# Gated linear attention: one head per half of the array's rows for scores and state, one product per decay level for q and k together, the output gate read from PSUM

## The chip, the cores and the metric

The kernel runs on one core of a Trainium2 chip, as one launch. The metric is the device time of that launch in microseconds (us). The engines are TensorE (PE, matrix products), VectorE (DVE), ScalarE (ACT), GpSimd (POOL) and SyncE (SP, which here issues transfers). Each has its own instruction stream, and semaphores order them. A tile is spread over 128 partitions; PE writes its results to PSUM, which has eight banks.

## The reference

One step of a layer with two groups of heads side by side, followed by a feed-forward part:

```
n = rmsnorm(x);  z = n @ w_in
A = windowed attention with sinks          (8 heads)
B = gated linear attention (GLA)           (4 heads, 64 keys by 128 values)
h = x + concat(A, B) @ w_out
y = h + relu(rmsnorm(h) @ w_up)^2 @ w_down
```

The change is in the GLA. Per chunk, with `g` the log of the forget gate of each key channel:

```
b     = cumsum(g)
o     = (q * exp(b)) @ S + A @ v
A[t,s] = sum_k q[t,k] * k[s,k] * exp(b[t,k] - b[s,k])   for s <= t
S_new = exp(b[-1]) * S + (k * exp(b[-1] - b))^T @ v
out   = rmsnorm_per_head(o) * g_gla_out * silu(rg)
```

There are 2048 prompt tokens (16 tiles of 128) and 32 sample tokens (tile 16, which runs first).

## The kernel before, in words

The program has three phases: projections and attention to about 401 us, the GLA (`gla_phase`) from there to about 772 us, then the output projection and the feed-forward part. The GLA goes through eight halves h of two tiles (the first also has the sample tile). Per half PE projects q and k (`zq`, `zk`: four results of 24 products with 256 columns, `gla_cols`), `decay` makes the running sum `cc` of the log gates, and per tile PE projects v (`zv`: 24 products with 512 columns).

Two heads lie one above the other on the 128 partitions (64 key channels each), and there are two such pairs p. `gla_tile` handles one tile:

- L767 and L772: `qkp` = q * k (the diagonal of A) and `Qc` = q * exp(b), on DVE.
- The decay factors. For each level m of 64, 32, ... 1 the tokens are cut into blocks of 2m, and the score of a row in the second half of a block against a column in its first half is factored at the block's middle. POOL makes the exponents of the two halves of the blocks apart (L788, L789) and those of the state update (L779) in tiles `E` of four levels; ACT takes the exponential in place (L113).
- DVE then multiplies q by E into `Qb` (L798, 14 instructions per tile, one for each level and head, 64 partitions each). `Qb` is block-diagonal: each head's part lies beside zeros, so that one product over all 128 rows gives two heads. DVE also multiplies E by k in two instructions of 1024 columns (L804).
- PE: `dg` (the diagonal), `kdp` (transposes for the state update), then the scores `A0`, `A1`: 26 products, in tiles of 128 rows by 64 columns, 64 moving columns each (128 for m = 64). Each f32 product is two instructions in the trace.
- DVE copies the scores under a mask into `AT` (L863, `copy_predicated`, 12 per tile); ACT does the level m = 64 (L856).
- PE: `go` (the output: `Qc` times the state with 256 columns, `AT` times v with 128) and `dS` (L879 to L890); DVE updates the state `Sp` (L896, four instructions on 64 partitions); ACT copies and squares the output (L901, L902), DVE sums the squares (L904), takes the inverse root (L170 to L175) and multiplies into the gate `g` (L909, four instructions); PE transposes it (`gTp`), and a transfer takes it out.

The order of the work: tasks (`gla_tile`, `decay`) are generators that yield for so many ns on a clock of PE work that the builder keeps (`_pe`, `tick`, `finish`), so PE's instructions stand in the order in which the builder emits them, and a PE instruction that waits holds all behind it. The other engines' orders are set by a scheduler. PSUM has three banks for the wide projections and five for everything else in this phase (`ps_s`), handed out in turn: a new tile waits until the last reader of the one five before it is done. `reach` and `after` make a tile wait in the builder for a stage of an earlier one.

Of the kernel before, what the change touches and what calls it, by code (L numbers as in the profile page):

```python
# [13 lines left out]
ALU = mybir.AluOpType  # L14
# [14 lines left out]
class Builder:  # L29
# [630 lines left out]
    def gla_phase(self):  # L660
        tc, a, V, S, G, Q = self.tc, self.a, self.V, self.S, self.G, self.Q
        nt = self.nt
        with ExitStack() as ctx:
# [7 lines left out]
            for key in ("p", "s"):  # L671
                St[key] = c.tile([P, 2, 2, P], F32, tag=f"S{key}", name=f"S{key}")
                G.memset(St[key], 0.0)
            Qb = [c.tile([P, 7, 2, 2, 64], F32, tag=f"Qb{i}", name=f"Qb{i}") for i in range(2)]
            for x in Qb:
                G.memset(x, 0.0)
            for p in range(2):
                for hh in range(2):
                    Q.dma_start(St["s"][hh * 64 : hh * 64 + 64, p, hh, :], a["state_gla"][2 * p + hh])

            halves = self.halves
            vs, gs, vready, cnt, glas, stage, decs = {}, {}, set(), [0], [], {}, {0: self.dec0}
# [18 lines left out]
            def project(h):  # L701
# [3 lines left out]
                qg = wk.tile([P, 2, 288], F32, tag="qg", name=f"qg_{h}")  # L705
                kg = wk.tile([P, 2, 288], F32, tag="kg", name=f"kg_{h}")
                for wt, dst, sc, nm in ((self.wqg, qg, 0.125, "q"), (self.wkg, kg, 1.0, "k")):
                    for p in range(2):
                        if h == 0 and self.head0:
                            ps = self.head0.pop(0)  # L710
                        else:
                            ps = self.gla_cols(wt, p, f"z{nm}_{h}_{p}", rh, rl, N)
                        V.scalar_tensor_tensor(out=dst[:, p, :N], in0=ps, scalar=sc, in1=rb[:, :N], op0=ALU.mult, op1=ALU.mult)
# [5 lines left out]
                offs = np.cumsum([0] + [self.rows(t) for t in tiles])  # L719

                for i, t in enumerate(tiles):
                    r = self.rows(t)
                    if i < 2:
                        n = len(glas)
                        reach(n - 2, 2)
                        glas.append(None)
                        glas[n] = self.spawn(gla_tile(n, t, int(offs[i]), qg, kg, self.cc[h]), 0 if i else 0)
                        self.tick()
# [9 lines left out]
                    if i == 2:  # L738
# [3 lines left out]
                        glas[n] = self.spawn(gla_tile(n, t, int(offs[i]), qg, kg, self.cc[h]), 0)  # L742
# [11 lines left out]
            def gla_tile(n, t, off, qg, kg, cc):  # L754
# [5 lines left out]
                q, k, cv = qg[:, :, tk], kg[:, :, tk], cc[:, :, tk]  # L760
# [3 lines left out]
                Qt = Qb[cnt[0] % 2]  # L764
                cnt[0] += 1
# [8 lines left out]
                for gi, g_ in enumerate([list(range(0, 4)), list(range(4, NL + 1))]):  # L774
                    E = wk.tile([P, 4, 2, P], F32, tag="E", name=f"E_{t}_{gi}", bufs=4)
                    for s_, li in enumerate(g_):
                        ev = E[:, s_, :, :L]
                        if li == NL:
# [3 lines left out]
                            continue  # L782
                        m = lv[li]
                        nb = L // (2 * m)
                        c5 = cv.rearrange("q p (n h m) -> q p n h m", h=2, m=m)
                        e5 = ev.rearrange("q p (n h m) -> q p n h m", h=2, m=m)
                        ref = c5[:, :, :, 0, m - 1 : m].broadcast_to([P, 2, nb, m])
# [4 lines left out]
                    for s_, li in enumerate(g_):  # L792
                        if li == NL:
                            continue
                        m = lv[li]
                        for hh in range(2):
                            hp = slice(hh * 64, hh * 64 + 64)
                            (G if li % 4 < 0 else V).tensor_tensor(  # L798
                                out=Qt[hp, li, :, hh, : L // 2].rearrange("q p (n m) -> q p n m", m=m),
                                in0=q[hp].rearrange("q p (n h m) -> q p n h m", h=2, m=m)[:, :, :, 1, :],  # L800
                                in1=E[hp, s_, :, :L].rearrange("q p (n h m) -> q p n h m", h=2, m=m)[:, :, :, 1, :],
                                op=ALU.mult,
                            )
# [26 lines left out]
                for p in range(2):  # L830
                    self.tr(pk[:L, p * P : (p + 1) * P], kd[:, p, :L])
# [4 lines left out]
                for gi, (l0, l1) in enumerate(((0, 3), (3, 7)) if L == P else ((0, NL),)):  # L836
                    ps = self.ps_s(f"A{gi}_{t}")
                    at, c0 = {}, 0
                    for li in range(l0, l1):
                        w = 64 if lv[li] == 64 else L // nh // 2  # L840
                        at[li] = ps[:, c0 : c0 + 4 * w].rearrange("s (p h x) -> s p h x", p=2, h=2)
                        c0 += 4 * w
                        for p in range(2):
                            if w == 64:

                                self.mm(at[li][p * 64 : p * 64 + 64, p], K(li)[:, p, :64], Qt[:, li, p], True, True)
                                continue
                            for a0 in range(nh):
                                r = slice(a0 * 64, a0 * 64 + L // nh)
                                self.mm(at[li][r, p], K(li)[:, p, r], Qt[:, li, p, :, a0 * w : (a0 + 1) * w], True, True)  # L850
                    for li in range(l0, l1):
                        m = lv[li]
                        w = at[li].shape[3]
                        if m == 64:
                            for p in range(2):
                                S.activation(AT[:64, 2 * p : 2 * p + 2, 64:], at[li][p * 64 : p * 64 + 64, p], AF.Copy)  # L856
                            continue
                        for a0 in range(nh):
                            r = slice(a0 * 64, a0 * 64 + L // nh)
                            dst = AT[r, :, r].rearrange("s a (n h m) -> s a n h m", h=2, m=m)[:, :, :, 1, :]  # L860
                            src = at[li][r].rearrange("s p h (n m) -> s (p h) n m", m=m)
                            mk = masks[r, LEVELS.index(m), :w].rearrange("s (n m) -> s n m", m=m)
                            V.copy_predicated(dst, mk.unsqueeze(1).broadcast_to([L // nh, 4, w // m, m]), src)  # L863
                    if l1 < NL:
                        yield 800
# [10 lines left out]
                o = self.ps_s(f"go_{t}")  # L876
                for p in range(2):
                    if not first:
                        self.mm(  # L879
                            o[:L, p * 256 : p * 256 + 256], Qc[:, p, :L], St_[:, p].rearrange("k h v -> k (h v)"), True, False  # L880
                        )
# [523 lines left out]
```

## Time and profile before

| What | Value |
|---|---|
| Three runs, us | 2366.48, 2371.55, 2370.27 (median 2370.27) |
| The profiled execution, us | 2372.48 |
| Its span, us | 2370.7 |
| Granted TensorE clock, mean | 0.979 |
| PE busy over the span | 95% |
| DVE, ACT, POOL busy | 63%, 40%, 50% |

The profiled execution is 2.2 us above the median of the runs; 1.8 us of its time lie around its span. A busy share over the whole span says little here: the phase after 772 us is PE's alone, while in the GLA the engines hand work to each other. The windows view gives busy times by stretch, the waits view what an engine stood still for, the lines view the mean duration of each kind of instruction, the timeline single instructions (a run of equal ones in one row, from the first start to the last end).

### The profile page before, as it was taken

The numbers are of one execution on the slowest core, as the hardware profiler recorded it, in microseconds if no ns is written. First come the engines' busy times: TensorE is split into PE (matmuls) and PEld (weight loads), VectorE is DVE, ScalarE is ACT, GpSimd is POOL, SyncE is SP. The second block draws the span as 40 slices with busy tenths as digits, with TensorE's granted clock in tenths as the row PEclk, the third lists the DMA queues.
The fourth block names the chain that finished last, engine by engine and source line by source line (L and its number), as shares of the span: only waits on it lengthen the run. The fifth ranks groups of instructions, "written<-read, shape, count | busy, mean of one in ns | idle before, by whom it ended". The sixth has DMA issues, their size and how long they took to land.

```text
span 2370.7 us, 38100 instructions
## 1 busy us (share of the span) xinstructions
PE 2246.4 (95%) x14473; PEld 2112.0 (89%) x14473; DVE 1501.8 (63%) x3621; ACT 949.4 (40%) x2011; POOL 1187.1 (50%) x1074
## 2 busy tenths in 40 slices
PE   6999999898877899999999899999999999999999
PEld 4777776687767899999999899999999999999999
DVE  6665656999999755555564755555556665555555
ACT  3554444454543633333334533333334533333331
POOL 3221224333341457766754466666663556666662
PEclk9999999899998999999999999999999999999999
DMA  8864563322322422232226222222226122222221
GB/s 204 159 126 103 129 165 120 82 75 59 102 80 74 121 81 72 81 98 72 72 86 193 80 71 72 72 72 71 71 62 223 35 82 72 72 72 72 72 63 51
DMA packets 214455, 221.45 MB, mean 93 GB/s; under 512 B 38736, under 2 KB 178976, under 8 KB 214272
## 3 DMA queue, kind: packets, MB, share of 16 engines
q1 hardware_dynamic: 214272, 219.02, 33.4%
q8 instruction: 114, 1.87, 0.3%
q14 instruction: 69, 0.57, 0.1%
HBM read 180.08 MB, written 38.91 MB: 92 GB/s over the span
## 4 chain that ended last, share of the span: by engine, by line
PE 76%; DVE 14%; DMA 4%; ACT 2%; issue 1%; POOL 1%; SPq 1%; POOLq 0%; ACTq 0%; DVEq 0%
PE dn L105 30%; PE op L105 6%; PE PS4B L105 4%; PE PA11B L105 4%; PE PA12B L105 4%; PE zq L105 4%; PE PS1T L105 3%; PE PA22T L105 3%; PE PS3T L105 3%; PE PS2T L105 3%; PE zr L105 3%; DVE Qb L798 3%; DVE AT L863 2%; PE zkv L105 2%; PE zv L105 2%
## 5 line engine op out<-in xcount | busy, mean ns | idle before, releaser
L1073 POOL TENSOR_TENSOR wu<-stage,wu 128x512 fp32r<-128x512 f32 x336 | 435.1, 1304 | 514.3 <-ACT wu L1072 514.3
L1240 DVE TENSOR_TENSOR y<-y,dn 128x360 f32<-128x360 f32 (+1 forms) x768 | 392.2, 514 | 221.4 <-PE dn L105 218.4
L1072 ACT ACTIVATE wu<-stage 128x512 fp32r<-128x512 f32 x336 | 205.9, 627 | 491.8 <-PE dn L105 224.7
L1075 POOL TENSOR_TENSOR stage<-stage 128x512 f32<-128x512 f32 x192 | 250.5, 1304 | 7.5
L1193 ACT ACTIVATE r<-PA11B 128x360 f32<-128x360 f32 (+1 forms) x48 | 22.0, 458 | 315.7 <-PE PA11B L105 315.7
L1180 DVE TENSOR_TENSOR PA12B<-PA12B,r 128x360 f32<-128x360 f32 (+1 forms) x48 | 25.3, 527 | 150.2 <-PE PA12B L105 150.2
L105 PE MATMUL PS2T<-T2h,wu 128*128 128x360 f32 (+1 forms) x384 | 100.7, 324 | 13.9 <-ACT T2h L1105 13.9
L699 POOL TENSOR_TENSOR g<-g,ggla 128x512 f32<-128x512 f32 (+1 forms) x17 | 22.8, 1347 | 170.5 <-ACT g L113 170.5
L105 PE MATMUL PA22T<-T4h,wu 128*128 128x360 f32 (+1 forms) x384 | 102.8, 332 | 0.0
L105 PE MATMUL PS4B<-B22h,wu 128*128 128x360 f32 (+1 forms) x384 | 100.0, 324 | 0.0
L105 PE MATMUL PS3T<-T3h,wu 128*128 128x360 f32 (+1 forms) x384 | 99.4, 322 | 0.0
L105 PE MATMUL PS1T<-T1h,wu 128*128 128x360 f32 (+1 forms) x384 | 98.9, 321 | 0.0
L105 PE MATMUL PA11B<-B11h,wu 128*128 128x360 f32 (+1 forms) x384 | 98.8, 321 | 0.0
L105 PE MATMUL PA12B<-B21h,wu 128*128 128x360 f32 (+1 forms) x384 | 98.7, 321 | 0.0
L798 DVE TENSOR_TENSOR Qb<-qg,E 64x128 f32<-64x128 f32 (+1 forms) x234 | 86.7, 370 | 10.5 <-ACT E L113 7.4
L105 PEld LDWEIGHTS PS2T<-T2h,wu 128*128 128x128 f32 x384 | 68.9, 190 | 14.8 <-ACT T2h L1105 14.8
L497 ACT ACTIVATE P<-S,negm 128x192 f32<-128x192 f32 (+2 forms) x128 | 51.5, 417 | 51.7 <-DVE negm L492 34.9
L863 DVE COPY_PREDICATED AT<-masks,A 64x128 f32<-64x128 int32 (+1 forms) x197 | 67.4, 342 | 6.2 <-ACT AT L856 1.2
L105 PEld LDWEIGHTS PA22T<-T4h,wu 128*128 128x128 f32 x384 | 71.2, 196 | 0.0
L105 PEld LDWEIGHTS PS4B<-B22h,wu 128*128 128x128 f32 x384 | 68.9, 190 | 0.0
L105 PEld LDWEIGHTS PS3T<-T3h,wu 128*128 128x128 f32 x384 | 68.6, 189 | 0.0
L105 PEld LDWEIGHTS PS1T<-T1h,wu 128*128 128x128 f32 x384 | 68.1, 188 | 0.0
(1008 smaller groups left out, 7807.0 us busy)
## 6 DMA issues: line engine op xcount, KB each, us to landing
stage<-in_w_up SPq DMA_DIRECT2D x96, 512.0 KB, 3.7
stage<-in_w_down SPq DMA_DIRECT2D x96, 512.0 KB, 3.9
stage<-in_w_out SPq DMA_DIRECT2D x24, 512.0 KB, 4.8
xT1a<-in_xT_prompt SPq DMA_DIRECT2D x16, 512.0 KB, 4.1
stage<-in_w_in SPq DMA_DIRECT2D x16, 512.0 KB, 6.7
x1a<-in_x_prompt SPq DMA_DIRECT2D x16, 512.0 KB, 6.6
out_yT_prompt<-y SPq DMA_DIRECT2D x32, 180.0 KB, 2.6
m<-mixT SPq DMA_DIRECT2D x11, 512.0 KB, 3.9
```

What stands on the lines that cost most here:

```text
L105: self._pe(self.T.matmul(out, lhsT, rhs, start=start, stop=stop), ns)
L497: S.activation(Pt[:, u, :n], sp[:, jp], AF.Exp, bias=negm[:, ch, u : u + 1], scale=0.125, accum_out=rsum[:, ch, u : u + 1],)
L699: G.tensor_tensor(out=gv, in0=gv, in1=ggla[:r].unsqueeze(1).broadcast_to([r, 4, P]), op=ALU.mult)
L798: (G if li % 4 < 0 else V).tensor_tensor(out=Qt[hp, li, :, hh, : L // 2].rearrange("q p (n m) -> q p n m", m=m), in0=q[hp].rearrange("q p ...
L863: V.copy_predicated(dst, mk.unsqueeze(1).broadcast_to([L // nh, 4, w // m, m]), src)
L1072: S.activation(h, src, AF.Copy)
L1073: G.tensor_tensor(out=l, in0=src, in1=f32(h), op=ALU.subtract)
L1075: tt = lambda o, x, y, op: G.tensor_tensor(out=o, in0=x, in1=y, op=op)
L1180: tt = lambda out, x, y, op=ALU.add: V.tensor_tensor(out=out, in0=x, in1=y, op=op)
L1193: S.activation(r0, product(b, "A11", "B11"), AF.Copy)
L1240: V.tensor_tensor(out=yg[:, f, :], in0=yg[:, f, :], in1=ps, op=ALU.add)
```

## The change

All of it is in `gla_phase`.

- q and k of a half are stored in one tile `kq`, tile after tile of tokens, k beside q.
- POOL makes each level's exponents in one subtraction of 256 columns (b minus b at the block's middle, sign not handled); ACT takes the absolute value of four levels in one more pass, and its exponential has the scale -1/16.
- DVE multiplies in place, one instruction of 256 columns per level: k where the token is in the first half of a block, q in the second (`halves_of`). The two products of 1024 columns and `Qb` with its zeros are gone; the factor of the state update has a product of its own.
- PE's scores: one head per instruction, 64 rows by 64 columns, heads alternating, into a bank each (`A0` for the upper head, `A1` for the lower): 52 products of 32 moving columns (64 for m = 64) in place of 26. The moving operand is read from E with strides.
- `copy_predicated`: 20 per tile of 64 x 64 in place of 12 of 64 x 128; the level m = 32 goes to ACT (four copies more).
- The state `St` has no zeros beside it. `Qc` times the state is four products of 128 columns with 64 rows each, in place of two of 256 columns with 128 rows, into two banks `go0` and `go1`. `dS` keeps its four products. DVE updates the state in two instructions.
- ACT squares each head from PSUM with a running sum (four instructions, each with a read of the sum); its copy of the output and DVE's reduction are gone. The four gate products read `go0` and `go1` in PSUM.

No transfer is added or taken away.

```diff
-            Qb = [c.tile([P, 7, 2, 2, 64], F32, tag=f"Qb{i}", name=f"Qb{i}") for i in range(2)]
...
-                        G.tensor_tensor(out=e5[:, :, :, 0, :], in0=ref, in1=c5[:, :, :, 0, :], op=ALU.subtract)
-                        G.tensor_tensor(out=e5[:, :, :, 1, :], in0=c5[:, :, :, 1, :], in1=ref, op=ALU.subtract)
+                        c4, e4 = (x.rearrange("q p (n u) -> q p n u", u=2 * m) for x in (cv, ev))
+                        ref = c4[:, :, :, m - 1 : m].broadcast_to([P, 2, L // (2 * m), 2 * m])
+                        G.tensor_tensor(out=e4, in0=c4, in1=ref, op=ALU.subtract)
                     ng = len(g_)
-                    self.table(E[:, :ng, :, :L], E[:, :ng, :, :L], AF.Exp, scale=1.0 / 16)
+                    S.activation(E[:, :ng], E[:, :ng], AF.Abs)
+                    self.table(E[:, :ng], E[:, :ng], AF.Exp, scale=-1.0 / 16)
                     for s_, li in enumerate(g_):
+                        ev = E[:, s_]
                         if li == NL:
+                            V.tensor_tensor(out=ev, in0=ev, in1=k, op=ALU.mult)
                             continue
                         m = lv[li]
-                        for hh in range(2):
-                            hp = slice(hh * 64, hh * 64 + 64)
-                            (G if li % 4 < 0 else V).tensor_tensor(
-                                out=Qt[hp, li, :, hh, : L // 2].rearrange("q p (n m) -> q p n m", m=m),
...
-                    V.tensor_tensor(
-                        out=E[:, :ng, :, :L], in0=E[:, :ng, :, :L], in1=k.unsqueeze(1).broadcast_to([P, ng, 2, L]), op=ALU.mult
-                    )
+                        e4 = ev.rearrange("q p (n h m) -> q (p n) h m", h=2, m=m)
+                        V.tensor_tensor(out=e4, in0=e4, in1=halves_of(kq, L, m), op=ALU.mult)
...
-                                self.mm(at[li][r, p], K(li)[:, p, r], Qt[:, li, p, :, a0 * w : (a0 + 1) * w], True, True)
+                            for hh in range(2):
+                                x = K(li)[hh * 64 : hh * 64 + 64, p]
+                                q2 = x[:, s1]
+                                if m < 64:
+                                    q2 = q2.rearrange("q (n h m) -> q n h m", h=2, m=m)[:, :, 1, :]
+                                self.mm(at[li][hh][s0, p], x[:, s0], q2, True, True)
...
-                        self.mm(
-                            o[:L, p * 256 : p * 256 + 256], Qc[:, p, :L], St_[:, p].rearrange("k h v -> k (h v)"), True, False
-                        )
+                        for hh in range(2):
+                            hp = slice(hh * 64, hh * 64 + 64)
+                            self.mm(o[hh][:, p], Qc[hp, p, :L], St_[hp, p], True, False)
...
-                S.activation(v[:L], o[:L], AF.Copy)
-                S.activation(sq[:L], o[:L], AF.Square)
+
                 ss = self.small.tile([P, 4], F32, tag="ssg", name=f"ssg_{t}")[:L]
-                V.reduce_sum(ss, sq[:L].rearrange("p (h v) -> p h v", h=4), axis=AX.X)
+                for hd in range(4):
+                    cs = slice(hd * P, (hd + 1) * P)
+                    S.activation(sq[:L, cs], o[hd % 2][:, hd // 2], AF.Square, accum_out=ss[:, hd : hd + 1])
...
-                        out=g[:L, cs], in0=v[:L, cs], scalar=rs[:, hd : hd + 1], in1=g[:L, cs], op0=ALU.mult, op1=ALU.mult
+                        out=g[:L, cs], in0=o[hd % 2][:, hd // 2], scalar=rs[:, hd : hd + 1], in1=g[:L, cs], op0=ALU.mult, op1=ALU.mult
```

DVE's order between the scores of tile 7 and the state after tile 6, before (`AT_7` the masked copies, `Qb` the q products of tile 8, `Sp` the state that `go_7` on PE waits for):

```order
L863 COPY_PREDICATED AT_7_6380<-masks_2828,A1_7_6468 64x4x4x8 x2
L798 TENSOR_TENSOR Qb1_4494<-qg_4_6288,E_8_0_6582 64x2x64
L863 COPY_PREDICATED AT_7_6380<-masks_2828,A1_7_6468 64x4x8x4
L798 TENSOR_TENSOR Qb1_4494<-qg_4_6288,E_8_0_6582 64x2x64 x2
L863 COPY_PREDICATED AT_7_6380<-masks_2828,A1_7_6468 64x4x8x4
L798 TENSOR_TENSOR Qb1_4494<-qg_4_6288,E_8_0_6582 64x2x64 x5
L863 COPY_PREDICATED AT_7_6380<-masks_2828,A1_7_6468 64x4x16x2 x2
L713 SCALAR_TENSOR_TENSOR kg_4_6289<-zk_4_0_6431,rb_4_5795 128x256
L863 COPY_PREDICATED AT_7_6380<-masks_2828,A1_7_6468 64x4x32 x2
L798 TENSOR_TENSOR Qb1_4494<-qg_4_6288,E_8_1_6601 64x2x64 x6
L896 SCALAR_TENSOR_TENSOR Sp_4489<-Sp_4489,ec_6_6092,dS_6_6526 64x128 x4
```

and in the changed kernel:

```order
L869 COPY_PREDICATED AT_7_6555<-masks_2828,A0_7_6618 64x2x8x4 x2
L869 COPY_PREDICATED AT_7_6555<-masks_2828,A1_7_6619 64x2x8x4 x2
L869 COPY_PREDICATED AT_7_6555<-masks_2828,A0_7_6618 64x2x16x2 x2
L869 COPY_PREDICATED AT_7_6555<-masks_2828,A1_7_6619 64x2x16x2 x2
L869 COPY_PREDICATED AT_7_6555<-masks_2828,A0_7_6618 64x2x32 x2
L869 COPY_PREDICATED AT_7_6555<-masks_2828,A1_7_6619 64x2x32 x2
L900 SCALAR_TENSOR_TENSOR Sp_4489<-Sp_4489,ec_6_6254,dS_6_6728 128x128 x2
L908 TENSOR_SCALAR ssg_6_6735<-ssg_6_6735 128x4
```

The state update now stands directly behind the copies; the decay products of tiles 8 and 9 come later. There the gate products of tile 6, which read the banks `go0_6` and `go1_6`, stand in DVE's order behind those of tile 8 and two of tile 9:

```order
L804 TENSOR_TENSOR E_8_0_6797<-E_8_0_6797,kq_4_6426 128x256 x3
L804 TENSOR_TENSOR E_8_1_6808<-E_8_1_6808,kq_4_6426 128x256 x3
L800 TENSOR_TENSOR E_8_1_6808<-E_8_1_6808,kq_4_6426 128x256
L772 TENSOR_TENSOR qkp_9_6886<-kq_4_6426 128x256
L804 TENSOR_TENSOR E_9_0_6892<-E_9_0_6892,kq_4_6426 128x256 x2
L912 SCALAR_TENSOR_TENSOR g_6_5997<-go0_6_6718,rsq_y_g6_6741,g_6_5997 128x128
L912 SCALAR_TENSOR_TENSOR g_6_5997<-go1_6_6719,rsq_y_g6_6741,g_6_5997 128x128
L912 SCALAR_TENSOR_TENSOR g_6_5997<-go0_6_6718,rsq_y_g6_6741,g_6_5997 128x128
L912 SCALAR_TENSOR_TENSOR g_6_5997<-go1_6_6719,rsq_y_g6_6741,g_6_5997 128x128
```

Before, these four read a copy in SBUF (`v`). The banks are now held until DVE is through them, and `dg_8` and `kdp_8` on PE are the next users of the two.

## Rows read from the trace of the kernel before

**Rows 1.** Windows: stretch, length, busy of PE, PEld, DVE, ACT, POOL, PEclk, DMA.

```profile
445.00:500.60 55.60, 46.04 (x384) 39.94 (x385) 51.58 (x158) 21.80 (x40) 20.32 (x47) 0.87 0.23 62
...
582.53:623.30 40.77, 36.14 (x321) 30.88 (x321) 37.46 (x114) 20.18 (x37) 14.68 (x32) 1.00 0.28 82
...
704.00:745.00 41.00, 26.64 (x194) 22.45 (x194) 39.82 (x92) 12.64 (x25) 13.42 (x15) 0.79 0.19 54
```

**Rows 2.** PE's waits in 400 to 520: us in total, times, longest.

```profile
PE go L105 <- DVE Sp L896: 5.6, 1, 5.6
PE go L105 <- DVE AT L863: 5.4, 1, 5.4
...
PE kdp L109 <- DVE AT L863: 2.7, 1, 2.7
```

**Rows 3.** PE's waits in the half 582.53 to 623.30, both ends counted.

```profile
PE go L105 <- DVE Sp L896: 4.1, 2, 2.0
...
PE gTp L109 <- DVE g L909: 0.7, 1, 0.7
```

**Rows 4.** Timeline of DVE ahead of 583 us: start, us, instruction, count.

```profile
579.32 2.35 DVE L798 TENSOR_TENSOR Qb<-qg,E 64x128 f32<-64x128 f32 x6
581.68 1.45 DVE L896 SCALAR_TENSOR_TENSOR Sp<-Sp,ec,dS 64x128 f32<-64x128 f32 x4
```

**Rows 5.** Timeline of PE, DVE and POOL, 702 to 727, idle before and releaser.

```profile
715.62 1.19 PE L105 MATMUL go<-Sp,Qc 128*128 128x256 f32 x2 [12.84 <-DVE Sp L896]
...
726.49 0.40 PE L105 MATMUL dg<-ones,qkp 128*64 128x2 f32 x8 [0.74 <-DVE qkp L767]
...
702.16 10.49 DVE L798 TENSOR_TENSOR Qb<-qg,E 64x128 f32<-64x128 f32 x1
...
711.89 0.62 POOL L779 TENSOR_TENSOR E<-cc 128x256 f32<-128x256 f32 x1
```

**Rows 6.** DVE by line and form, 410 to 775: busy us, mean ns.

```profile
L798 DVE TENSOR_TENSOR Qb<-qg,E 64x128 f32<-64x128 f32 x224 | 84.8, 379 | 10.4 <-ACT E L113 7.4
L863 DVE COPY_PREDICATED AT<-masks,A 64x128 f32<-64x128 int32 x192 | 66.2, 345 | 6.1 <-ACT AT L856 1.2
L804 DVE TENSOR_TENSOR E<-E,kg 128x1024 f32<-128x1024 f32 x32 | 39.9, 1264 | 0.1
...
L767 DVE TENSOR_TENSOR qkp<-qg,kg 128x256 f32<-128x256 f32 x15 | 6.2, 417 | 0.1
...
L863 DVE COPY_PREDICATED AT<-masks,A 32x64 f32<-32x64 int32 x5 | 1.2, 239 | 0.1
```

**Rows 7.** ACT by line and form, 410 to 775.

```profile
L113 ACT ACTIVATE E<-E 128x1024 f32<-128x1024 f32 x31 | 32.1, 1050 | 20.3 <-POOL E L779 12.3 <-POOL E L789 7.9
...
L856 ACT ACTIVATE AT<-A 64x128 f32<-64x128 f32 x32 | 8.6, 268 | 1.3 <-PE A L105 0.8
```

**Rows 8.** ACT by line and form, whole span: reads of a running sum.

```profile
L497 ACT ACTIVATION_READ_ACCUMULATOR P<-S,negm 128x1 f32 x128 | 26.5, 207 | 0.0
```

**Rows 9.** PE by line and form, 410 to 775.

```profile
L105 PE MATMUL dg<-ones,qkp 128*64 128x2 f32 x128 | 6.5, 204 | 8.2 <-DVE cc L649 5.6 <-DVE AT L863 1.9 <-DVE qkp L767 0.7
```

**Rows 10.** Timeline of PE: scores of tile 6; output of one tile.

```profile
526.60 1.84 PE L105 MATMUL A<-Qb,E 128*64 128x128 f32 x52
...
583.04 0.61 PE L105 MATMUL go<-v,AT 128*128 128x128 f32 x4
583.48 0.60 PE L105 MATMUL go<-Sp,Qc 128*128 128x256 f32 x2
583.91 0.61 PE L105 MATMUL go<-v,AT 128*128 128x128 f32 x4
```

**Rows 11.** Timeline of PE in the attention: two row halves alternating.

```profile
311.13 0.29 PE L105 MATMUL zkv<-wkvh,nT_12l 128*128 128x272 f32 x1
311.35 0.92 PE L105 MATMUL S<-kW,qT 64*128 64x192 f32 x8
312.20 0.39 PE L105 MATMUL zkv<-wkvh,nT_12h 128*128 128x272 f32 x1
```

More of the change, by code (lines that the diff above doesn't have):

```diff
@@ L704, in project @@
                 rh, rl = (lambda kb: nh[:, kb, :N]), (lambda kb: nl[:, kb, :N])
-                qg = wk.tile([P, 2, 288], F32, tag="qg", name=f"qg_{h}")
-                kg = wk.tile([P, 2, 288], F32, tag="kg", name=f"kg_{h}")
-                for wt, dst, sc, nm in ((self.wqg, qg, 0.125, "q"), (self.wkg, kg, 1.0, "k")):
+                kq = wk.tile([P, 4 * 288], F32, tag="kq", name=f"kq_{h}")
+                offs = np.cumsum([0] + [self.rows(t) for t in tiles])
+                runs = [(0, 1, NS)] * (len(tiles) == 3) + [(N - 2 * P, 2, P)]
+                for wt, x, sc, nm in ((self.wqg, 1, 0.125, "q"), (self.wkg, 0, 1.0, "k")):
                     for p in range(2):
@@ L712, in project @@
                             ps = self.gla_cols(wt, p, f"z{nm}_{h}_{p}", rh, rl, N)
-                        V.scalar_tensor_tensor(out=dst[:, p, :N], in0=ps, scalar=sc, in1=rb[:, :N], op0=ALU.mult, op1=ALU.mult)
+                        for at, j, L in runs:
+                            dst = kq[:, 4 * at : 4 * (at + j * L)].rearrange("q (j x p t) -> q x p j t", j=j, x=2, p=2)[:, x, p]
+                            src, rbs = (y[:, at : at + j * L].rearrange("q (j t) -> q j t", j=j) for y in (ps, rb))
+                            V.scalar_tensor_tensor(out=dst, in0=src, scalar=sc, in1=rbs, op0=ALU.mult, op1=ALU.mult)
                 wvg = self.wvg
@@ L718, in project @@
                 self.finish(decs[h])
-                offs = np.cumsum([0] + [self.rows(t) for t in tiles])
                 for i, t in enumerate(tiles):
@@ L752, in after, with halves_of, gla_tile @@
                 reach(n, s)
-            def gla_tile(n, t, off, qg, kg, cc):
+            def halves_of(kq, L, m):
+                a = kq[:, 0, 0]
+                return bass.AP(a.tensor, a.offset, [a.ap[0], [2 * m, L // m], [2 * L + m, 2], [1, m]])
+            def gla_tile(n, t, off, kq, cc):
                 stage[n] = 0
@@ L759, in gla_tile @@
                 tk = slice(off, off + L)
-                q, k, cv = qg[:, :, tk], kg[:, :, tk], cc[:, :, tk]
+                kq, cv = kq[:, 4 * off : 4 * (off + L)].rearrange("q (x p t) -> q x p t", x=2, p=2), cc[:, :, tk]
+                k, q = kq[:, 0], kq[:, 1]
                 lv = [m for m in LEVELS if m < L]
@@ L835, in gla_tile @@
                 nh = max(1, L // 64)
[L836 to L849, printed above, removed]
-                                self.mm(at[li][r, p], K(li)[:, p, r], Qt[:, li, p, :, a0 * w : (a0 + 1) * w], True, True)
-                    for li in range(l0, l1):
-                        m = lv[li]
-                        w = at[li].shape[3]
+                pa = [self.ps_s(f"A{hh}_{t}") for hh in range(2)]
@@ new lines, in gla_tile @@
+                at, c0 = {}, 0
+                for li, m in enumerate(lv):
+                    w = 64 if m == 64 else L // nh // 2
+                    at[li] = [x[:, c0 : c0 + 2 * w].rearrange("s (p x) -> s p x", p=2) for x in pa]
+                    c0 += 2 * w
+                    for p in range(2):
+                        for a0 in range(nh if m < 64 else 1):
+                            s0, s1 = (slice(0, 64), slice(64, P)) if m == 64 else (slice(a0 * 64, a0 * 64 + L // nh),) * 2
+                            for hh in range(2):
[4 more added lines that the diff above has]
+                                self.mm(at[li][hh][s0, p], x[:, s0], q2, True, True)
+                    if li == 2:
+                        yield 300
@@ L854, in gla_tile @@
+                A4 = AT.rearrange("s (p h) t -> s p h t", p=2)
+                for li, m in enumerate(lv):
+                    for hh in range(2):
+                        src = at[li][hh]
                         if m == 64:
-                            for p in range(2):
-                                S.activation(AT[:64, 2 * p : 2 * p + 2, 64:], at[li][p * 64 : p * 64 + 64, p], AF.Copy)
+                            S.activation(A4[:64, :, hh, 64:], src[:64], AF.Copy)
                             continue
@@ L893, in gla_tile @@
                 for p in range(2):
[L894 to L902 removed]
+                    V.scalar_tensor_tensor(
+                        out=St_[:, p], in0=St_[:, p], scalar=ec[:, p, L - 1 : L], in1=ds[:, p], op0=ALU.mult, op1=ALU.add
+                    )
                 ss = self.small.tile([P, 4], F32, tag="ssg", name=f"ssg_{t}")[:L]
[L904 removed]
+                for hd in range(4):
+                    cs = slice(hd * P, (hd + 1) * P)
+                    S.activation(sq[:L, cs], o[hd % 2][:, hd // 2], AF.Square, accum_out=ss[:, hd : hd + 1])
                 V.tensor_scalar(out=ss, in0=ss, scalar1=1.0 / P, scalar2=EPS, op0=ALU.mult, op1=ALU.add)
```

64 lines of the change are left out of this document (26 added, 38 removed).

## The prediction

> **What bounds the kernel now.** I read the windows first. In a steady half PE is busy for 36.1 of 40.8 us and DVE for 37.5, and the clock is granted in full (1.00, the 2.4 GHz level); ACT has 20 and POOL 15 [rows 1]. So both PE and DVE are near their limit there. Between 445 and 500.6 us DVE is busy for 51.6 of 55.6 us and PE for 46.0, at a mean granted clock of 0.87; near the end, 704 to 745, PE has 26.6 of 41 at 0.79 [rows 1]. These two stretches are where PE stands still. The waits say for what: at the start for the state update (5.6), the masked copies (5.4 and 2.7), all on DVE [rows 2]; in a steady half 2.0 us for the state update (the row counts both ends of the half, one belongs to it) and 0.7 for the gate [rows 3]; near the end 12.84 us once for the state update [rows 5]. The timeline shows the reason: ahead of the state update DVE still does the q products of the next tile [rows 4], and at 702.16 a single one of these took 10.49 us, against a mean of 0.38 for its kind, while POOL's backlog of subtractions ran to 712.5 [rows 5, 6]. So the change has to be judged by what it takes off DVE ahead of the state update, and by what it adds to PE, which is the next bound.
>
> **DVE.** Per prompt tile it loses 14 q products of 0.379 (5.31), 2 products with k of 1.264 (2.53) and 12 masked copies of 0.345 (4.14): 11.98 us [rows 6]. It gains 8 products of 256 columns and 20 masked copies of 64x64. The nearest row for a product is `qkp`, same size, 0.417; for a copy the 32x64 one, 0.239 [rows 6]. That is 3.34 + 4.78 = 8.12, so 3.9 less per tile and 7.7 per half, which leaves DVE under 30 of 40.8 us. The upper bound: strides could make a product twice a 64x128 q product with its strides (0.76) and a copy as dear as the larger one (0.345); that is 6.1 + 6.9 = 13.0, 1 us more than now. I take the lower prices, since size sets the time in the two copy rows and the q product's 0.379 holds stretches like the 10.49. The two state updates saved and the reduction saved I leave unpriced, as a reserve. What matters more is the order: the state update now stands directly behind the copies, with no decay product ahead of it.
>
> **ACT and POOL.** ACT gains two passes for the absolute value at 1.050, four copies at up to 0.268 [rows 7], and four squares with a read of 0.207 each [rows 8] in place of a copy and a square: with 0.268 a square at most 2.1 + 1.1 + 1.9 = 5.1 per tile, 10 per half, so under 31 of 40.8. POOL gets 8 subtractions of some 0.62 [rows 5] for 15 smaller ones; its backlog gets shorter. Neither is the bound; I cost them at nothing. The cover is that decay factors are made a tile or two ahead; without it, each absolute value is 1.05 us on the path. No transfer moves, so SP's queue is as before.
>
> **PE, scores.** Now 104 instructions instead of 52. The old 52 took 1.84 us [rows 10], with 64 columns each. The row for `dg`, with 2 columns, shows what an instruction costs when it has almost no columns: eight in 0.40 [rows 5], of which one alone takes 0.204 [rows 9], so (0.40 - 0.20)/7 = 0.028 from one to the next. By columns: the four of 128 columns in the output begin 0.44 us ahead of what follows them [rows 10], 0.11 each, so 32 columns alone need 0.028 and 64 need 0.055. The old scores went at about 0.03 each, half of 0.055, so two column halves ran side by side. Forecast: 103 x 0.028 + 0.2 = 3.1 us, 1.25 more per tile. Upper bound 0.055 (halving the columns buys nothing and no two run together): 5.7, or 3.9 more. No row shows less than 0.028, so no gain.
>
> The Trainium skill's page TensorEngine Tiling (Array Packing), section Instruction Overhead, speaks against this part: a matmul carries about 60 cycles whatever its columns, one with 1 column takes as long as one with 60, and a tiling factor should not be taken from a dimension that is already small. At 2.4 GHz that is an estimate of 25 ns, so 2.6 us for 104; the `dg` row, at 28, agrees with it.
>
> **PE, output.** Per pair, two instructions of 256 columns (0.43 [rows 10]) become four of 128 in alternating row halves. In the attention eight such instructions of 192 columns took 0.85 us to the next start [rows 11]; alone they would need 8 x 0.165 = 1.3. So row halves do run together, and four need between 0.22 (all overlapped) and 0.44. But PE has to go to 64-row tiles and back twice per tile; around the eight of the attention the gap was 0.22 before their first [rows 11]. Per tile that is -0.4 + 2 x 0.1 to 0.3; without overlap up to +0.6. I take +0.1.
>
> **The sum.** Steady part (500 to 704 us, five halves): -2.0 - 0.7 + 2 x (1.25 + 0.1) = 0.0 per half. The waits go, and PE's extra instructions fill them. Here the kernel gains nothing. A wait of `dg` for the running sum of the gates stays.
>
> Start (five tiles): the three waits, -13.7, go, since DVE has 3.9 less per tile. The 46.0 busy us at 0.87 would be 40 at full clock; without long stands I take 5 of these 6 back. Extra PE work is 5 x 1.35 = 6.8. Together -12.
>
> End: the 12.84 goes, but what is late next is the gate: `dg_14` takes the bank that the gate products of tile 12 read, and these stand behind decay products of tiles 14 and 15. POOL's last subtraction of that backlog ended at 712.5 [rows 5]; taken as the latest time now too, two passes of ACT (2.1), two products (0.8) and four gate products at the same price (1.7) put the gate's end at 717, an estimate. So `dg_14` comes at some 717.5 instead of 726.5 [rows 5], -9, and the last two tiles pay 2 x 1.35 = 2.7: -6.
>
> Sum -18: the profiled execution would go from 2372.5 to 2354.5. The median of the runs is 2.2 lower than that execution, so **2352**.
>
> **The rivals.**
>
> *PE takes it all back* (no change). Each ns on the price of a score instruction costs 17 x 104 = 1768 instructions, 1.8 us. At 38 ns instead of 28 the 18 us are gone: about 2370. For it: the moving operand is read with strides from a wide tile, which no row shows. Against: columns need 28 ns alone and may overlap.
>
> *The scores go one after the other* (slower). At 55 ns, the upper bound, the extra is 27 x 1.77 = 48: 2352 + 48 = 2400. It decides from 38 ns on. For it: every instruction alternates its row half, with new weights each time. Against: the attention's eight alternate too and overlap [rows 11].
>
> *The banks are held* (new wait). `dg_8` and `kdp_8` wait for the gate of tile 6, behind ACT's longer chain. In a steady half I count some 3 us of slack. If the gate comes 3 us later than that in all seven halves, 21 us are lost: about 2373. For it: ACT gains 10 us per half ahead of it; against: DVE gets 7.7 faster.
>
> *DVE stays shut out* (a smaller gain). The 10.49 us are not a matter of how much DVE does; while POOL runs back to back, an instruction of DVE with two operands in SBUF may stand as long, whichever it is. Then half of the start's 12 and all of the end's 6 stay away: about 2364. For it: the products still read two SBUF operands. Against: POOL has half the instructions, and the state update reads PSUM.
>
> The Trainium skill's page SBUF — State Buffer, section Who interferes with whom, has the shared ports locked for one whole instruction when both engines read SBUF. By that rule the stand would be about one POOL subtraction long, and the gain of the start and the end would be had in full; the 10.49 us of the trace are longer than one such (0.62), so the trace does not agree, and the measurement decides.
>
> **How the numbers follow.** About 0.2%, some 5 us, is what a measurement here can tell from no change. Forecast 0.52, own range 2338 to 2362 (start 6 to 18 less, end 2 to 11 less, and up to 3 from the unpriced reserve). Shut out 0.15. Taken back 0.14. One after the other 0.11. Banks held 0.08, half of it within no change, half slower. Faster: 0.52 + 0.15 = 0.67, and 0.01 of the taken-back case; same 0.13 + 0.04 = 0.17; slower 0.11 + 0.04 = 0.15. The range leaves out most of the case at 2400 and a little below: 2335 to 2376.
>
> **What would show it.** Right: scores of a tile in 2.9 to 3.4 us; no wait of `go` for the state update over 1 us in a steady half, whose length stays at 40 to 41; DVE under 30 busy per half; the stretch 445 to 500 with a clock over 0.95; `go_13` early and `dg_14` waiting for the gate. Wrong: score instructions over 38 ns, `dg` or `kdp` waiting for the gate in steady halves, a decay product of many us beside POOL.

## The result, and the profile after

The changed kernel takes 2378.01 us (median of 6 runs, 2376.23 to 2381.09) against 2370.14 for the kernel before (6 runs): ratio 1.0035, 95% interval 1.0022 to 1.0048. It is slower by some 8 us, where 18 us less were forecast, and lies above the range of 2335 to 2376. The profiled execution has a span of 2379.3 us, 8.6 more than before.

Where the 8.6 us come from is read from one mark, the start of `dg` on PE, which every tile has once. The timelines of the two kernels (and of the experiment `e7_order`, below) give, in us:

| Start on PE | before | changed | difference | e7_order | difference |
|---|---|---|---|---|---|
| `dg` of tile 4 | 512.08 | 502.89 | -9.2 | 499.73 | -12.4 |
| `dg` of tile 12 | 671.66 | 684.65 | +13.0 | 659.48 | -12.2 |
| `dg` of tile 14 | 726.49 | 732.86 | +6.4 | 705.72 | -20.8 |
| end of the span | 2370.7 | 2379.3 | +8.6 | 2351.5 | -19.2 |

So the start gained 9 us (forecast 12). The stretch from tile 12 to tile 14 gained some 7 and the last two tiles lost 2, so the end gained 4 (forecast 6). The loss is all in the middle: 22 us in four halves, where the forecast was nothing. The windows of these four halves, from `dg` of tile 4 to `dg` of tile 12, before and changed:

```profile
512.08:671.66 159.58, 143.59 (x1282) 123.22 (x1281) 146.17 (x442) 81.19 (x148) 59.18 (x128) 1.00 0.30 83
```

```profile
502.89:684.65 181.76, 158.96 (x1729) 136.33 (x1728) 117.26 (x431) 104.28 (x244) 48.06 (x72) 0.89 0.28 79
```

PE's waits (those over 0.15 us) sum to 16.0 us in the first and 22.8 in the second, 7 more. The other 15 us are PE itself, busy for 159.0 us instead of 143.6 at a mean granted clock of 0.89 instead of 1.00. Seven stretches at 0.50, the 1.2 GHz level, make up 41 us of the second window, each beginning close to one of the waits below, and the first window has none. So by this count two thirds of the loss is the lower clock at the waits, one third their length.

The windows of the changed kernel, the stretches of [rows 1]:

```profile
445.00:500.60 55.60, 51.49 (x483) 43.10 (x482) 42.47 (x151) 31.60 (x75) 14.90 (x23) 0.85 0.25 69
...
582.53:623.30 40.77, 34.90 (x405) 29.29 (x404) 25.59 (x95) 24.78 (x59) 12.08 (x18) 0.94 0.29 83
...
704.00:745.00 41.00, 38.06 (x427) 32.79 (x426) 29.84 (x93) 26.37 (x61) 21.00 (x22) 0.92 0.28 86
```

DVE fell from 37.5 to 25.6 us in the middle one, ACT rose from 20.2 to 24.8; none is full. Yet a half takes 45.0 us there (`dg` of tile 8 at 593.02, of tile 10 at 637.97), against 40.8 before; over that half DVE is busy for 29.3 us and ACT for 26.1. PE's waits in 500 to 690 us, changed kernel (us in total, times, longest):

```profile
PE dS L105 <- ACT gT L921: 11.5, 3, 4.0
PE dg L105 <- DVE cc L649: 7.4, 4, 2.4
PE go L105 <- ACT kdT L831: 3.9, 2, 3.2
```

(`gT` is ACT's copy of `gTp`, `kdT` its copy of `kdp`.) In the same stretch of the kernel before:

```profile
PE go L105 <- DVE Sp L896: 14.5, 5, 5.6
PE dg L105 <- DVE cc L649: 5.6, 3, 1.9
PE gTp L109 <- DVE g L909: 2.2, 3, 0.7
...
```

The waits for the state update and the gate are gone, as forecast. In their place PE waits for ACT, which it had not done there. The timeline of ACT shows what stands ahead of the copies. Before, in one half:

```profile
567.91 0.36 ACT L833 ACTIVATE kdT<-kdp 128x256 f32<-128x256 f32 x1
568.42 0.57 ACT L856 ACTIVATE AT<-A 64x128 f32<-64x128 f32 x2
569.01 0.60 ACT L918 ACTIVATE gT<-gTp 128x512 f32<-128x512 f32 x1
571.67 1.06 ACT L113 ACTIVATE E<-E 128x1024 f32<-128x1024 f32 x1 [2.06 <-POOL E L789]
```

and in the changed kernel, same place of the program:

```profile
567.58 1.06 ACT L795 ACTIVATE E<-E 128x1024 f32<-128x1024 f32 x1 [2.31 <-POOL E L793]
568.67 1.06 ACT L113 ACTIVATE E<-E 128x1024 f32<-128x1024 f32 x1
569.64 0.37 ACT L831 ACTIVATE kdT<-kdp 128x256 f32<-128x256 f32 x1
569.90 1.05 ACT L795 ACTIVATE E<-E 128x1024 f32<-128x1024 f32 x1
570.98 1.06 ACT L113 ACTIVATE E<-E 128x1024 f32<-128x1024 f32 x1
573.43 1.06 ACT L795 ACTIVATE E<-E 128x1024 f32<-128x1024 f32 x1 [1.40 <-POOL E L793]
574.40 0.25 ACT L858 ACTIVATE AT<-A 64x128 f32<-64x128 f32 x1
574.55 0.20 ACT L864 ACTIVATE AT<-A 32x64 f32<-32x64 f32 x1
...
575.62 0.60 ACT L921 ACTIVATE gT<-gTp 128x512 f32<-128x512 f32 x1
```

The order has turned round. The decay passes of the next two tiles, which wait for POOL twice, now stand ahead of the score copies of tile 7 and of the copy of `gTp`. No run shows why the scheduler turned them round. What that does is in the timelines of PE and DVE:

```profile
566.24 1.82 PE L105 MATMUL A<-E 64*64 64x64 f32 x104
...
568.82 0.60 PE L109 MATMUL gTp<-packed,g 128*128 128x128 f32 x4
...
576.27 1.12 PE L105 MATMUL dS<-v,kdT 128*64 128x128 f32 x8 [4.03 <-ACT gT L921]
```

```profile
575.17 5.68 DVE L869 COPY_PREDICATED AT<-masks,A 64x64 f32<-64x64 int32 x20 [8.71 <-ACT AT L864]
580.88 0.61 DVE L900 SCALAR_TENSOR_TENSOR Sp<-Sp,ec,dS 128x128 f32<-128x128 f32 x2
```

The scores were there at 568.1. DVE's masked copies into the same tile wait for ACT's copies and begin at 575.2; `dS` waits for the bank that `gTp` held, until ACT has read it. The state update is directly behind the copies on DVE, as the order rows promised, but the copies are 7 us late.

### The profile page after: what moved, and what is told of

It reads as the page before. It is cut to its first block, busy times and chain, and to the rows that moved or that the text cites. A ratio compares the mean times of both kernels' runs of the same rounds, so it can differ in the third digit from the quotient of the medians.

```text
span 2379.3 us, 39960 instructions
## 1 busy us (share of the span) xinstructions
PE 2269.6 (95%) x15389; PEld 2131.7 (90%) x15389; DVE 1414.3 (59%) x3573; ACT 996.0 (42%) x2211; POOL 1159.6 (49%) x954
## 4 chain that ended last, share of the span: by engine, by line
PE 80%; DVE 9%; DMA 4%; ACT 4%; POOL 2%; issue 2%; SPq 0%; POOLq 0%; ACTq 0%; DVEq 0%
PE dn L105 30%; PE op L105 6%; PE PS4B L105 4%; PE PA11B L105 4%; PE PA12B L105 4%; PE zq L105 4%; PE PS2T L105 3%; PE PS1T L105 3%; PE PA22T L105 3%; PE PS3T L105 3%; PE zr L105 3%; PE zv L105 3%; PE zkv L105 2%; DVE AT L869 2%; PE zk L105 1%
## 5 line engine op out<-in xcount | busy, mean ns | idle before, releaser
L869 DVE COPY_PREDICATED AT<-masks,A 64x64 f32<-64x64 int32 (+1 forms) x330 | 82.5, 252 | 76.6 <-ACT AT L864 63.6
L793 POOL TENSOR_TENSOR E<-cc 128x256 f32<-128x256 f32 (+1 forms) x117 | 68.3, 618 | 24.4 <-PE A L105 19.0
```

The costliest lines, as they stand in the source:

```text
L793: G.tensor_tensor(out=e4, in0=c4, in1=ref, op=ALU.subtract)
```

## The experiments

Each was timed against the kernel before on the same chip; ratios below 1 are faster. The changed kernel has its own runs of the kernel before, so differences to it are read from the ratios (0.001 is 2.4 us). Theory A is the one above: ACT's order. B is the number of PSUM banks in use per half (18 against 16), C the four ACT copies of level m = 32 alone, D the pass for the absolute value alone.

**e1_m32_dve**: the level m = 32 back on DVE.

```diff
-                            if m == 32:
-                                r1, r2 = slice(r.start, r.start + 32), slice(r.start + 32, r.stop)
-                                S.activation(A4[r1, :, hh, r2], src[r1], AF.Copy)
-                                continue
```

> The changed kernel with one part undone: the level m = 32 of the scores goes into AT by DVE's masked copy again (24 per tile), not by four copies of ACT. In the changed kernel DVE stood 72.8 us ahead of its masked copies, 63.6 of them for these ACT copies. Theory A (ACT's order: tile 7's copies and the copy of gTp stand behind the decay passes of tiles 8 and 9, which wait for POOL): DVE no longer waits, so dg comes earlier, but dS still waits some 4 us per half for the copy of gTp; about 2370, a half of it back. Theory C (the four ACT copies are the whole loss): no dS wait over 1 us either, about 2352. Theory B (the loss is PSUM banks): no change, 2378.

Measured: 2376.85 us, ratio 1.0033 (1.0018 to 1.0048). No gain; C is out. A's number (2370) was missed too, because DVE then waits for ACT's copy of the level m = 64 instead, which stands as late. DVE's group of masked copies in 500 to 690 us, with its idle time before them:

```profile
L865 DVE COPY_PREDICATED AT<-masks,A 64x64 f32<-64x64 int32 x192 | 47.9, 250 | 52.0 <-ACT AT L858 46.5
```

**e2_ds_in_go**: `dS` in the free half of the bank of `go0`.

```diff
-                o = [self.ps_s(f"go{hh}_{t}")[:L, :256].rearrange("t (p v) -> t p v", p=2) for hh in range(2)]
+                ob = [self.ps_s(f"go{hh}_{t}") for hh in range(2)]
+                o = [x[:L, :256].rearrange("t (p v) -> t p v", p=2) for x in ob]
...
-                ds = self.ps_s(f"dS_{t}")[:, :256].rearrange("k (p v) -> k p v", p=2)
+                ds = ob[0][:, 256:].rearrange("k (p v) -> k p v", p=2)
```

> The changed kernel with dS in the free half of the bank of go0, so without a bank of its own (16 tiles of a bank per half as in the kernel before, not 18). Theory B (more banks per half, so that dS waits for the bank of gTp): the dS waits of 3.9 and 4.0 us per half go and nothing comes instead, about 2350. Theory A (ACT's order): dS no longer waits itself, but DVE's masked copies still stand behind ACT, so the state update and go come late instead; 2365 to 2380.

Measured: 2368.19 us, 0.9998 (0.9984 to 1.0013). The banks are a part, some 9 us of it, but not the 28 that B wanted. As A says, the wait of `dS` went and others came, among them the old one for the state update (500 to 690 us):

```profile
PE dg L105 <- DVE cc L649: 6.7, 4, 2.4
PE go L105 <- ACT kdT L831: 5.5, 3, 2.9
PE go L105 <- DVE Sp L901: 4.1, 2, 2.6
```

**e3_no_abs**: two subtractions per level with their sign on POOL, no absolute value on ACT.

```diff
-                        c4, e4 = (x.rearrange("q p (n u) -> q p n u", u=2 * m) for x in (cv, ev))
-                        ref = c4[:, :, :, m - 1 : m].broadcast_to([P, 2, L // (2 * m), 2 * m])
-                        G.tensor_tensor(out=e4, in0=c4, in1=ref, op=ALU.subtract)
+                        c5, e5 = (x.rearrange("q p (n h m) -> q p n h m", h=2, m=m) for x in (cv, ev))
+                        ref = c5[:, :, :, 0, m - 1 : m].broadcast_to([P, 2, L // (2 * m), m])
+                        G.tensor_tensor(out=e5[:, :, :, 0, :], in0=ref, in1=c5[:, :, :, 0, :], op=ALU.subtract)
+                        G.tensor_tensor(out=e5[:, :, :, 1, :], in0=c5[:, :, :, 1, :], in1=ref, op=ALU.subtract)
...
-                    S.activation(E[:, :ng], E[:, :ng], AF.Abs)
-                    self.table(E[:, :ng], E[:, :ng], AF.Exp, scale=-1.0 / 16)
+                    self.table(E[:, :ng], E[:, :ng], AF.Exp, scale=1.0 / 16)
```

> The changed kernel with the exponents made with their sign again (two subtractions per level on POOL), so without ACT's pass for the absolute value. ACT loses 2.1 us per tile, POOL gains some 1.5. Here the copies of tile 7 and of gTp stand ahead of tile 9's pass but still behind tile 8's two. Theory A: the ACT copies wait for less, dS waits 1 to 2 us instead of 4; about 2362. Theory D (ACT's load alone matters): back to 2352. Theory B: 2378.

Measured: 2376.72 us, 1.0030 (1.0018 to 1.0042). No gain: D's 2352 did not come, and A's 2362 was too hopeful. Tile 8's two passes still stand ahead of the copies there, and `dS` still waits up to 3.3 us for the copy of `gTp`. Since the edit also lengthens POOL's list, for which the passes wait, it is no clean test of D; `e14_order_noabs` below tries it again.

**e7_order**: the same instructions; the decay passes are held behind the last score copy and the last copy of `gTp`, and tile 8's passes are given out only when tile 7's copies have been. PE's and POOL's orders are the same row for row; on DVE some instructions changed places too.

```diff
-                    S.activation(E[:, :ng], E[:, :ng], AF.Abs)
+                    if gi == 0:
+                        t0c = self.clock
+                        if t % 2 == 0 and t != nt:
+                            yield from after(n - 1, 2)
+                    ab = S.activation(E[:, :ng], E[:, :ng], AF.Abs)
+                    for x in [*self.last_copies.values(), self.last_table]:
+                        self.tc.add_manual_dep(ab.ins, x.ins.name, NOSYNC, reason="copies first")
...
-                yield 9000
+                yield max(0, t0c + 9000 - self.clock)
...
-                            S.activation(A4[:64, :, hh, 64:], src[:64], AF.Copy)
+                            self.last_copies['A'] = S.activation(A4[:64, :, hh, 64:], src[:64], AF.Copy)
...
-                                S.activation(A4[r1, :, hh, r2], src[r1], AF.Copy)
+                                self.last_copies['A'] = S.activation(A4[r1, :, hh, r2], src[r1], AF.Copy)
...
-                S.activation(gT[:, :, :L], pg, AF.Copy)
+                self.last_copies['gT'] = S.activation(gT[:, :, :L], pg, AF.Copy)
...
+            self.last_copies = {}
```

> The changed kernel with one thing different, the order on ACT: the decay passes of a half's two tiles are put behind the last masked-score copies and the last copy of gTp that stand ahead of them in the program; the same instructions, PE's order the same row for row. Theory A: the waits of dS for gT (3.9 to 4.0 us per half) and DVE's wait for ACT's copies go, a steady half falls from 45 to under 41 us, the clock there is back over 0.95; about 2350, faster than the kernel before. Theory B or C: no change within 5 us of 2378. Rival E: the decay passes come later, so that the gate products behind them hold the banks go0 and go1, and dg waits for the gate: 2365 to 2385.

Measured: 2352.22 us, 0.9925 (0.9900 to 0.9950): 26 us less than the changed kernel by order alone. ACT there, in the same half:

```profile
559.77 0.27 ACT L864 ACTIVATE AT<-A 64x128 f32<-64x128 f32 x1 [1.46 <-PE A L105]
559.95 0.20 ACT L870 ACTIVATE AT<-A 32x64 f32<-32x64 f32 x1
560.05 0.25 ACT L864 ACTIVATE AT<-A 64x128 f32<-64x128 f32 x1
560.32 0.68 ACT L870 ACTIVATE AT<-A 32x64 f32<-32x64 f32 x3
561.04 0.60 ACT L927 ACTIVATE gT<-gTp 128x512 f32<-128x512 f32 x1
561.53 1.05 ACT L799 ACTIVATE E<-E 128x1024 f32<-128x1024 f32 x1
```

and all that PE waits for in 500 to 690 us:

```profile
PE dg L105 <- DVE cc L649: 11.9, 5, 4.5
```

A is right: no wait for ACT, the state update or the gate is left in this stretch. A steady half is 39.9 us (578.66 to 618.57). The expected clock of 0.95 was not reached, 0.92; see below. Rival E's wait came once, behind this stretch: `dg` of tile 14 waits 4.06 us for the gate.

**e13_order_copies**: the same, but only the score copies are put first, not the copy of `gTp`.

> As e7_order, but only the masked-score copies are put ahead of the decay passes; the copy of gTp may fall between them (in tile 8's half it stands behind three passes). If the copies' place alone is worth the gain: 2352, and dS waits for gT at most 1 to 2 us. If the bank that dS gets from gTp is worth half of it: about 2365, with dS waiting 3 us or more per half.

Measured: 2356.84 us, 0.9956 (0.9942 to 0.9971). The place of the score copies is most of it, 19 us of the 26; `dS` still waits for ACT once, 1.9 us.

**e14_order_noabs**: `e7_order` without the absolute value, as in `e3_no_abs`.

> e7_order without the absolute value (two subtractions per level on POOL, with their sign). The prediction costed ACT's pass at nothing, being covered. If it is covered where ACT's order is right: 2349 to 2356, as e7_order. If ACT's load was the loss and the order only hid it: 2345 or less. If POOL's longer list (14 instead of 7 subtractions a tile) sets the pace: 2358 or more.

Measured: 2353.72 us, 0.9948 (0.9931 to 0.9966), as `e7_order`. So with ACT's order right no cost of the extra pass can be seen, which is what the prediction had said of it, and D is out.

**e15_order_ds**: `e7_order` and `e2_ds_in_go` together.

> e7_order and dS in the free half of go0's bank. Theory A: with ACT's order mended the banks are not short, 2348 to 2355. Theory B: 2342 or less, since both gains (26 and 10) add up.

Measured: 2345.18 us, 0.9907 (0.9892 to 0.9921), the best kernel of the study: 0.9% faster than the kernel before. Between the two expectations; its interval overlaps that of `e7_order`, so that the bank adds something on top is likely from the medians, not shown.

Five kernels went after the wait that is left, that of `dg` for L649 (a reader of `la`, the product that `decay` starts from; `dg` takes its bank).

**e8_order_m32** (`e7_order` and `e1_m32_dve`) and **e9_order_m32_ds** (that and `e2_ds_in_go`):

> The kernel with ACT's order mended (e7_order) and, beside that, the level m = 32 on DVE again (e1_m32_dve). With ACT's order mended DVE still stood 2.3 and 5.8 us ahead of its masked copies for ACT's four copies of m = 32, and behind these copies stands L649, for which dg waits 2.35 and 1.34 us. If that chain sets the dg wait: dg waits under 1 us, the clock after it stays up, about 2344. If the wait is set by when la itself is there: no change, 2352.

> e8_order_m32 and dS in the free half of go0's bank (e2_ds_in_go). Theory A says that with ACT's order mended banks are no longer short: within 4 us of e8_order_m32. Theory B (banks): 6 us or more under it.

Measured: 2357.39, 0.9945 (0.9923 to 0.9967), and 2349.98, 0.9913 (0.9882 to 0.9945). The `dg` waits stay (10.4 and 12.3 us in 500 to 690), so they do not hang on the m = 32 copies. The difference of 7 between the two, where A allowed 4 and B asked for 6, speaks for the banks again; here too the intervals overlap.

**e10_order_y800** (`e7_order`, and a pause of 800 in the scores, so that `la` comes before their second part), **e11_order_m32_y800** (with m = 32 on DVE) and **e16_order_ds_y800** (with `dS` in `go0`'s bank):

```diff
                     if li == 2:
-                        yield 300
+                        yield 800
```

> e7_order with one more thing: the pause inside a tile's scores is 800 ns of the builder's clock as in the kernel before, not 300. By that alone PE does la and gTp between the two parts of tile 8's scores, as in the kernel before, not behind them, so 1.2 us of scores stand between la and dg_9, which waits for la's reader L649. If the stand of 1.3 to 2.4 us at dg and the 6 us at half clock (0.50 from 589 to 595) behind it cost the half 3 to 4 us: a steady half of 36 to 37 us instead of 40, about 2340. If L649 is late whatever PE does (DVE's copies stand ahead of it): no change, 2352.

> All three: ACT's order mended, m = 32 on DVE, the pause of 800. If the dg wait is the last stand of a steady half: no wait over 0.5 us there, clock over 0.98 from 500 to 690, a half of 36 us, about 2335. If either alone does it, equal to e8_order_m32 or e10_order_y800 within 3 us.

> e15_order_ds with the pause of 800 in the scores. In e10_order_y800 the dg wait went and the clock stayed up in one half (38.6 us), but the next tile's second part of scores then waited for dg's copy and gTp for the masked copies (4.9 us). With one bank fewer per tile in the rotation, other instructions get these banks: if the banks' turn made those waits, 2340 to 2346; if DVE's copies are late in any case, 2360 or more.

Measured: 2365.90, 0.9977 (0.9962 to 0.9991); 2374.29, 1.0019 (1.0003 to 1.0035); 2359.78, 0.9962 (0.9948 to 0.9975). All three are slower than their like with the pause of 300, and the 2335 to 2346 that were hoped for did not come. In `e10_order_y800` the `dg` wait did go but for one of 2.0 us, and one half took 38.6 us at full clock; but the next tile's scores and `gTp` then waited longer than was saved, for banks that DVE frees late (500 to 690 us):

```profile
PE gTp L109 <- DVE AT L875: 12.2, 4, 4.9
PE A L105 <- DVE dg L822: 7.2, 3, 4.0
PE dg L105 <- DVE cc L649: 2.0, 1, 2.0
```

The change itself had altered this place, which its description does not name: before, the pause was 800 and stood behind the copies of the first part; since, it is 300 and all copies are given out behind the second part. These runs try the length of the pause alone, not the place of the copies.

## Why the prediction was wrong

- **The step that failed is the one on ACT and POOL**: "Neither is the bound; I cost them at nothing. The cover is that decay factors are made a tile or two ahead". The sum of ACT's work was right in kind (26.1 us in the half from 593.02, under the 31 allowed). But the question was not how much ACT does, it was what stands ahead of what. An instruction there that waits for POOL holds short copies behind it for which PE and DVE wait. The changed order of ACT was to be seen before any run; I showed the rows of DVE, and none of ACT. `e7_order` shows the price: 26 us; of the 22 between the two marks 15 are waits of PE and 7 its busy time at the lower clock.
- **The waits that were to go went.** `go` no longer waits for the state update in the middle, and the start gained 9.2 us, 12.4 with ACT's order mended, for a forecast of 12. Tiles 12 to 14 gained 6.6 and 8.6, for 9, and the last two tiles lost 2.2 and 1.6, for 2.7.
- **The scores were mis-sized.** 104 instructions take 1.82 us, where 3.1 were forecast and 1.84 is what the 52 of before took [rows 10]. They cost nothing more. The floor of 28 ns was read from `dg`, which has tiles of 128 rows, and did not hold for these. The two rivals that rest on their price (taken back, one after the other) are out.
- **What filled the middle instead** is the lower clock. With ACT's order mended PE's waits between the two marks fall from 16.0 to 7.4 us, all 7.4 of them `dg` (5.6 before), but PE is busy for 152.3 us instead of 143.6, at 0.93 instead of 1.00. The window of `e7_order`, for the two above:

```profile
499.73:659.48 159.75, 152.34 (x1729) 131.37 (x1729) 118.99 (x430) 105.09 (x244) 48.48 (x72) 0.93 0.31 90
```

- **That the sum fits with the order mended is luck.** The whole span then changes by -19.2 us, for -18, and the middle by +0.2, for 0.0. But the sum has 17 x 1.25 = 21 us of dearer scores that never came; without them it would read -39. In the middle the lower clock took their place. In the start they balance the 5 us that were to come back from the clock: it was to be over 0.95 in 445 to 500 and was 0.85, in the changed kernel and in `e7_order`.
- **The output** came as forecast, near enough. Before, the first row and the `dS` behind the three rows of [rows 10]:

```profile
582.53 0.67 PE L105 MATMUL go<-Sp,Qc 128*128 128x256 f32 x2 [2.03 <-DVE Sp L896]
...
584.45 0.66 PE L105 MATMUL dS<-v,kdT 128*64 128x128 f32 x8
```

The changed kernel:

```profile
584.57 0.49 PE L105 MATMUL go<-Sp,Qc 64*128 64x128 f32 x4
584.99 0.71 PE L105 MATMUL go<-v,AT 128*128 128x128 f32 x4
585.63 0.49 PE L105 MATMUL go<-Sp,Qc 64*128 64x128 f32 x4
586.05 0.71 PE L105 MATMUL go<-v,AT 128*128 128x128 f32 x4
586.69 0.66 PE L105 MATMUL dS<-v,kdT 128*64 128x128 f32 x8
```

From the first row to `dS` 2.12 us, against 1.92 before: +0.2 per tile, for +0.1.

- **DVE's prices** held: a masked copy of 64x64 took 0.254 (taken: 0.239), a product 0.427 in 500 to 690 (taken: 0.417).
- **"Shut out"** came in a small form, near the end only. No stand like the 10.49 us is left, but in the changed kernel two of the six products of this row took 2.59 and 2.62 us, while POOL did two instructions of 2.45:

```profile
724.14 6.55 DVE L804 TENSOR_TENSOR E<-E,kq 128x256 f32<-128x256 f32 x6
```

```profile
724.42 4.90 POOL L198 TENSOR_TENSOR wo_01l<-stage,wo_01h 128x1024 fp32r<-128x1024 f32 x2 [4.32 <-ACT wo_01h L194]
```

- **"Banks held"** named the right kind of wait with the wrong holder. In the changed kernel it was not the gate that held a bank too long (0.3 us in all, at `dg` of tile 14) but ACT's copy of `gTp`, for `dS`. `e2_ds_in_go` prices it at 9 us there. With ACT's order mended the gate does hold one, where the prediction looked for it at the end; it stands behind two such products of 2.6 us:

```profile
705.72 0.60 PE L105 MATMUL dg<-ones,qkp 128*64 128x2 f32 x8 [4.06 <-DVE g L918]
```

## What to carry to other kernels

Before an engine that is half idle is costed at nothing, look at its order of instructions on both sides of the change: a short copy that others wait for, behind a long pass that itself waits, is on the critical path however idle the engine is. When a change removes a bottleneck and moves work onto another engine, hold the old order of the short copies by hand. And when a bank or a wait is taken away, ask who gets that bank next: in several of these kernels the saved wait came back in another place.

## What the runs showed that I had not expected

**Score instructions of 64 x 64 tiles run closer together than the floor taken from `dg`.** (1.82 - 0.22)/103, with 0.22 (the mean of one) for the last, is 16 ns from one to the next, under the 28 of `dg`. In the trace four of them mostly start within some 10 ns, and the next four some 60 ns after the first: instructions that alternate between the halves of the rows are taken up side by side. The Trainium skill's page TensorEngine Tiling (Array Packing), section Instruction Overhead, gives each matmul some 60 cycles and warns against a tiling taken from a small dimension. The prediction's estimate of 25 ns from it agrees with `dg`, not with these scores, and here the measurement decides; but twice the instructions of half the columns saved no time either (1.82 us against 1.84). What the Trainium skill's page says in its section Key Properties, that different tiles work in parallel, is what these starts show.

**The clock fell behind a shorter wait than one that it had outlasted.** Before, this wait did not lower the granted clock, which stayed at 1.00 through the half [rows 1]:

```profile
602.43 0.40 PE L105 MATMUL dg<-ones,qkp 128*64 128x2 f32 x8 [1.86 <-DVE cc L649]
```

In `e7_order` a wait of 1.34 us was followed by some 6 us at 0.50, the 1.2 GHz level:

```profile
589.13 0.59 PE L105 MATMUL dg<-ones,qkp 128*64 128x2 f32 x8 [1.34 <-DVE cc L649]
...
590.25 0.42 PE L105 MATMUL zq<-nTb_5h,wqgl 128*128 128x256 f32 x1
590.46 0.41 PE L105 MATMUL zq<-nTb_5h,wqgh 128*128 128x256 f32 x1
```

A product of `zq` begins 0.21 us after the one before it there, against 0.12 at full clock. What PE did ahead of the wait differs: before it was scores in tiles of 128 rows, here `la` and `gTp` after the scores of 64-row tiles. But that alone does not decide it. In the changed kernel a wait of 1.34 us stood behind the same rows, at 513.35, and the clock stayed at 1.00:

```profile
513.00:520.00 7.00, 6.65 (x93) 6.43 (x94) 6.51 (x20) 5.35 (x9) 1.43 (x2) 1.00 0.65 182
```

What decides it stays open.
